# Tail of the second request: row buffers in a pool of their own, gate and up in turn

## The chip, the cores and the metric

The kernel runs on one core of one Trainium2 chip. The core has a matmul engine (PE, with its weight loads shown apart as PEld), three engines for element work (DVE, ACT and POOL) and SP, whose queue issues most of the loads. The metric is the device time of one execution in microseconds, the median of the runs.

## The reference

One layer of a hybrid encoder runs on two requests with the same weights: a prompt P of 512 tokens and a sample S of 1024 tokens, 1024 channels each. The front of the layer (projection, a chunked state-space scan, a long convolution by FFT) isn't touched here. What follows is the tail, the same for both requests:

```python
mix = jnp.concatenate([y_ssd, y_hy], axis=-1) @ w_out          # 2048 -> 1024
h = h + group_rmsnorm(mix, norm_mix_post)
u = group_rmsnorm(h, norm_ffn_pre)
ff = (jax.nn.silu(u @ w_gate) * (u @ w_up)) @ w_down            # 1024 -> 2816 -> 1024
h = h + group_rmsnorm(ff, norm_ffn_post)
gate = jax.nn.sigmoid((group_rmsnorm(h, ple_norm_pre) @ w_ple_gate).astype(f32))
e = (p_l @ w_ple_proj).astype(f32)
h = h + group_rmsnorm((gate * e).astype(dtype), ple_norm_post)
```

Everything is f32, and both requests' outputs are returned.

## The kernel before

**Precision.** Every f32 operand of a product is split into a high part and the rest (`split_w` for weights: ACT makes `whi` at L278, POOL makes `wlo` at L279; `split_ps` for activations: ACT at L311, DVE at L312). A product is three matmuls, `mm3` at L287 to L289: high by high, high by low, low by high. Lines L287 to L289 are shared by all gemms of the tail, so the stages are told apart by the names of the tiles.

**Stages of the tail, in program order.** P: out-projection, FFN, ple (`post` with `ple_norm_post`), with tiles in the pools `tail_u` and `tail_p`. Then S, in groups of 512 tokens, in three pools that follow each other on the right side of SBUF:

- `out_s`: for each of the two groups, `out_group`. It multiplies the 16 row blocks of `mix_s` (read back from DRAM as `mx` tiles by SP, L1172, and split into `mh` and `ml`) with `w_out` in two column halves of 512 (`nch`), 192 matmuls of 512 columns each, and then runs `post`.
- `hid_s`: `gate_up`. The FFN's gate and up products are computed for two column blocks of 128 at a time (a pair; 11 pairs in all) by a scheme of seven block products over four quarter blocks a11, a21, a22, a12 of the weights and sums of them. The first two pairs are done for each group apart (4 calls, 256-wide matmuls, 84 of them to a product), the other nine for both groups at once (168 to a product). The weight blocks come into ten `raw` tiles by SP (L1201), the sums of weight blocks are made on DVE (L1194), gate and up run zipped: one step of the one, one of the other. The results are written as `hid_s` to DRAM (L1267).
- `end_s`: for each group, the down-projection (22 row blocks of `hid_s`, read back as `mx`), its `post`, and the ple.

**The post.** `post` takes the four accumulator tiles of 128 tokens (`acc`): square sum (ACT, L302), reciprocal root (DVE L294, POOL L295), scaling with the gain row (DVE, L1040), residual add (DVE, L1041; the residual is loaded by SP, L1031), store, a second norm (DVE, L319), eight transposes of 128 x 128 a tile on PE (L325), and then a `take`, which makes the seven sums of activation blocks that the scheme wants (`Sums`: DVE L138 for the differences, ACT L311 and DVE L312 for their split into `bh` and `bl`). In P's posts a plain split follows the transposes. The gain rows are loaded by SP (L307).

**What sets the order.** The code is written in order, and the framework places each instruction on its engine's queue by a simulated timeline; `post` is marked urgent, so that it is placed ahead of other work that is ready. Each engine then works its queue off strictly in that order. A tile of a pool can be written when all readers of its former owner are done, and a pool that takes the place of another waits until the tiles there are released. So `hid_s` can't begin before `out_s` is done, and `end_s` not before `hid_s`. Weights of all gemms but gate and up come through six slots `wst` and six each of `whi` and `wlo` (L272).

## Time and profile before

| what | us |
|---|---|
| median of 3 runs | 2953.61 (2950.01 to 2957.2) |
| profiled execution | 2953.8 |
| its span | 2952.0 |
| PE busy | 2693.9 (91% of the span) |
| DVE busy | 1803.0 |
| ACT busy | 1275.2 |
| POOL busy | 1475.6 |
| mean clock granted to PE | 0.953 |

A row of the profile's groups gives the line, the engine, the tiles written and read, the shape and the count, then the busy time and the mean of one in ns, then the idle time of the engine ahead of it and what ended it. In a timeline row the first number is the start in us from the span's start, the second the duration, and the bracket holds the idle time ahead and what ended it. A row of the table by stage gives the stretch, its length, the busy time and instructions of each engine, the granted PE clock, the DMA share and the GB/s moved.

### The profile page before, as it was taken

The page shows a single profiled execution, that of the slowest core. Times are in us where ns is not written, and L with a number is a line of the kernel's source. Part 1 is how long each engine was busy: PE and PEld are TensorE (multiplying, and loading weights), DVE is VectorE, ACT ScalarE, POOL GpSimd, SP SyncE. Part 2 cuts the span into 40 slices and gives each one's busy share as a digit, 9 for nine tenths or more (in the row PEclk, how much of TensorE's full clock was granted, in tenths as well). Part 3 has the DMA queues.
Part 4 walks back from the last instruction along what each step waited for, and adds up shares of the span by engine and source line. Part 5 has one row for each costly group of instructions (what it writes and reads, how often), then busy time and mean ns, then how long its engine had stood idle before and what let it go on. Part 6 is the DMA issues. An engine that isn't in the chain of part 4 may idle for free.

```text
span 2952.0 us, 41577 instructions
## 1 busy us (share of the span) xinstructions
PE 2693.9 (91%) x14696; PEld 2280.1 (77%) x14696; DVE 1803.0 (61%) x2905; ACT 1275.2 (43%) x2442; POOL 1475.6 (50%) x1147
## 2 busy tenths in 40 slices
PE   7999999999999989788888897959489999899998
PEld 5987898788887767677777776748489999878776
DVE  6767996976666968677776833452653333223445
ACT  4534445763234656622223243454543333335453
POOL 4445554434444456555555644533575444435564
PEclk8999999999999999899999998979699999999999
DMA  5544556653435586643333344645332222266755
GB/s 167 176 140 129 159 170 204 197 148 102 120 100 172 184 271 201 222 135 107 100 114 114 96 143 155 217 159 164 116 106 80 77 80 81 80 196 194 237 184 194
DMA packets 430667, 442.28 MB, mean 150 GB/s; under 512 B 26929, under 2 KB 331897, under 8 KB 428155
## 3 DMA queue, kind: packets, MB, share of 16 engines
q1 hardware_dynamic: 344523, 348.39, 39.0%
q10 hardware_dynamic: 79024, 61.88, 6.5%
q0 software_dynamic: 6912, 29.36, 2.5%
q8 instruction: 116, 1.90, 0.3%
q14 instruction: 92, 0.75, 0.1%
HBM read 347.59 MB, written 91.95 MB: 149 GB/s over the span
## 4 chain that ended last, share of the span: by engine, by line
PE 71%; DVE 15%; DMA 5%; issue 3%; POOL 3%; ACT 2%; SPq 0%; ACTq 0%; POOLq 0%; DVEq 0%
PE g L287 18%; PE g L288 18%; PE g L289 18%; PE a L288 3%; PE a L287 3%; PE a L289 3%; DVE b L743 2%; PE a L959 2%; PE a L686 1%; POOL wlo L279 1%; DVE b L678 1%; DVE E L601 1%; PE a L390 1%; PE a L614 1%; POOL rs_t L295 1%
## 5 line engine op out<-in xcount | busy, mean ns | idle before, releaser
L279 POOL TENSOR_TENSOR wlo<-wst,whi 128x512 fp32r<-128x512 f32 (+1 forms) x564 | 827.7, 1476 | 791.3 <-ACT whi L278 737.8
L278 ACT ACTIVATE whi<-wst 128x512 fp32r<-128x512 f32 (+1 forms) x564 | 351.3, 628 | 477.3 <-PE g L288 249.3
L287 PE MATMUL g<-uh,whi 128*128 128x512 f32 (+1 forms) x1232 | 495.1, 402 | 10.9 <-DVE acc L1108 5.5
L289 PE MATMUL g<-uh,wlo 128*128 128x512 f32 (+1 forms) x1232 | 493.6, 401 | 0.0
L288 PE MATMUL g<-ul,whi 128*128 128x512 f32 (+1 forms) x1232 | 493.1, 400 | 0.0
L287 PE MATMUL g<-bh,whi 128*128 128x256 f32 x1056 | 300.0, 285 | 28.6 <-DVE gt L1194 12.3
L289 PE MATMUL g<-bh,wlo 128*128 128x256 f32 x1056 | 299.8, 284 | 1.2 <-POOL wlo L279 1.1
L288 PE MATMUL g<-bl,whi 128*128 128x256 f32 x1056 | 299.5, 284 | 0.0
L312 DVE TENSOR_TENSOR ml<-mx,mh 128x512 fp32r<-128x512 f32 x152 | 118.8, 785 | 286.7 <-ACT mh L311 257.5
L287 PEld LDWEIGHTS g<-uh,whi 128*128 128x128 f32 x1232 | 234.7, 191 | 71.2 <-issue 15.6
L289 PEld LDWEIGHTS g<-uh,wlo 128*128 128x128 f32 x1232 | 234.0, 190 | 54.3 <-issue 5.8
L288 PEld LDWEIGHTS g<-ul,whi 128*128 128x128 f32 x1232 | 234.0, 190 | 53.6 <-issue 6.9
L279 POOL TENSOR_TENSOR wlo<-raw,whi 128x512 fp32r<-128x512 f32 x130 | 174.9, 1356 | 152.4 <-ACT whi L278 138.2
L379 DVE SCALAR_TENSOR_TENSOR cv<-g,cols,cv 128x510 f32<-128x510 f32 (+3 forms) x192 | 193.0, 1006 | 65.1 <-ACT cv L373 63.1
L287 PEld LDWEIGHTS g<-bh,whi 128*128 128x128 f32 x1056 | 203.4, 193 | 30.5 <-DVE gt L1194 13.2
L289 PEld LDWEIGHTS g<-bh,wlo 128*128 128x128 f32 x1056 | 203.8, 193 | 2.0 <-POOL wlo L279 2.0
L288 PEld LDWEIGHTS g<-bl,whi 128*128 128x128 f32 x1056 | 203.9, 193 | 0.0
L295 POOL TENSOR_TENSOR rs_t<-rs_t,nhalf 128x1 f32<-128x1 f32 (+2 forms) x112 | 115.1, 1031 | 168.6 <-DVE rs_t L294 167.2
L287 PE MATMUL g<-whi,uh 128*128 128x264 f32 (+1 forms) x576 | 192.0, 335 | 2.9 <-ACT uh L311 2.1
L311 ACT ACTIVATE mh<-mx 128x512 fp32r<-128x512 f32 x152 | 95.6, 631 | 228.2 <-PE g L288 165.0
L288 PE MATMUL g<-wlo,uh 128*128 128x264 f32 (+1 forms) x576 | 190.6, 331 | 0.0
L289 PE MATMUL g<-whi,ul 128*128 128x264 f32 (+1 forms) x576 | 189.1, 329 | 0.0
(316 smaller groups left out, 6100.4 us busy)
## 6 DMA issues: line engine op xcount, KB each, us to landing
wst<-in_w_in SPq DMA_DIRECT2D x192, 256.0 KB
wst<-in_w_down SPq DMA_DIRECT2D x132, 256.0 KB
wst<-in_w_out SPq DMA_DIRECT2D x96, 256.0 KB
mx<-hid_s SPq DMA_DIRECT2D x88, 256.0 KB
rw<-rows_s SPq DMA_DIRECT2D x32, 512.0 KB
mx<-mix_s SPq DMA_DIRECT2D x64, 256.0 KB
raw<-in_w_gate SPq DMA_DIRECT2D x52, 256.0 KB
raw<-in_w_up SPq DMA_DIRECT2D x52, 256.0 KB
```

What stands on the lines that cost most here:

```text
L278: nc.scalar.activation(hi, w, AF.Copy)
L279: (eng or nc.gpsimd).tensor_tensor(out=lo, in0=w, in1=hi.bitcast(F32), op=ALU.subtract)
L287: nc.tensor.matmul(ps, lh, rh, start=first, stop=False, skip_group_check=shared)
L288: nc.tensor.matmul(ps, lh, rl, start=False, stop=False, skip_group_check=shared)
L289: nc.tensor.matmul(ps, ll, rh, start=False, stop=last, skip_group_check=shared)
L295: nc.gpsimd.tensor_tensor(out=t[:, :w], in0=t[:, :w], in1=self.nhalf[:, :w], op=ALU.pow)
L311: self.nc.scalar.activation(hi, ps, AF.Copy)
L312: self.nc.vector.tensor_tensor(out=lo, in0=ps, in1=hi.bitcast(F32), op=ALU.subtract)
L379: nc.vector.scalar_tensor_tensor(out[:, a:b], ps[:, a + d:b + d], wcol(w), out[:, a:b], ALU.mult, ALU.add)
L390: nc.tensor.transpose(ps[:, j * 128:(j + 1) * 128], srcs[i + j], self.ident)
L743: V.tensor_tensor(out=o, in0=a, in1=b, op=op)
L959: nc.tensor.matmul(ps[:, r], iv[:, r0 + r, c], X[:, r0 + r, c], start=c == 0, stop=c == 1)
```

## The change

A pool `mix_s` with the tiles `mx` (2), `mh` (3) and `ml` (3) is opened on the right side ahead of P's tail and lives to the end; its tiles are the row buffers of both the out-projection and the down-projection. `out_s` is opened beside it, before P's tail, with a `junk` and a `wsum` of its own, and two `stage` tiles in place of four. `stream_gemm` becomes a generator that stops after each column half: the first half of group 0 is written ahead of P's ple. The gemm of group 1 is as before behind the post of group 0 in the code; `out_group` and `out_post` are apart now. In `gate_up`, the two single pairs of group 0 have their `wsum`, `gt` and `sc` in the tiles of `mix_s`; the others have them in `hid_s`. Gate and up are computed in turn: the last two of the seven steps of one product run beside the first two of the next. The weights come through `wst` (six slots, shared with the other gemms), the product is written over the `gt` tile, and each weight sum is made right after its inputs' last use. In `take` the differences read the PSUM tile for the second half of the rows, and eight ACT copies fall away in all. `end_s` has no `mx`, `mh` and `ml` of its own.

```diff
     def take(self, ps, k, t):
-        x = self.stage[t, k] = K.T(self.pool, [128, 4, 128], "stage")
-        nc.scalar.activation(x, ps, AF.Copy)
-        if k == 0 or t < 2:
+        if t < 2:
+            x = self.stage[t, k] = K.T(self.pool, [128, 4, 128], "stage")
+            nc.scalar.activation(x, ps, AF.Copy)
             return
...
+        if k == 0:
+            w = self.stage[t, 0] = K.T(self.pool, [128, 4, 128], "wsum")
+            diff(w, ps, b11)
+            put(1, b11)
+            put(5, w)
+            return
+        w = self.stage[t, 0]
+        put(3, ps)
+        diff(w, ps, w)
...
     def stream_gemm(self, rows, nk, wsrc, evac):
...
             for t in ORDER:
                 evac(nch, t, pss[t])
+            yield
...
-            a11, a21, a22, a12 = (self.T(pool, [128, 4, 128], "raw") for _ in range(4))
+            a11, a21, a22, a12 = (self.raw_w(w[k:k + 512, c * 128:(c + 1) * 128].rearrange(
+                "(k p) m -> p k m", p=128)) for c, k in ((m, 0), (m + 1, 0), (m + 1, 512), (m, 512)))
...
             mm(1, X, a11, True)
             r1 = copy()
+            s1 = add(a21, a22, ALU.add)
             yield
-            s1 = add(a21, a22, ALU.add)
             mm(5, Z, s1, True)
+            s2 = add(s1, a11, ALU.subtract)
             yield
...
-            for _ in zip(product(I["w_gate"][0], m, gs, gate), product(I["w_up"][0], m, gs, mul)):
-                pass
-
-        for gs, ms in (([0], (0, 2)), ([1], (0, 2)), ([0, 1], range(4, NF, 2))):
-            for m in ms:
-                pair(m, gs)
+            yield product(I["w_gate"][0], pool, m, us, gate)
+            yield product(I["w_up"][0], pool, m, us, mul)
+
+        old = None
+        for job in jobs:
+            for p in pair(*job):
+                for i in range(5):
+                    next(p)
+                    if old and i < 2:
+                        next(old)
+                old = p
...
+        with self.pool("mix_s", side="right") as mp, ExitStack() as right:
+            pm = tags(mp, ("mx", 2), ("mh", 3), ("ml", 3))
+            tr = right.enter_context(self.pool("out_s", side="right"))
+            po = pm | tags(tr, ("acc", 4), ("row", 2), ("t4", 2), ("junk", 1), ("stage", 2), ("wsum", 1))
+            with self.pool("tail_u") as tu, self.pool("tail_p") as tp:
...
+                u = self.ffn(P, 0, pl, u)
+                acc = self.new_acc(po)
+                out = self.out_group(S, 0, po, acc)
+                next(out)
+                self.ple_post(P, 0, pl, self.ple(P, 0, pl, u))
...
+            next(out)
...
+                us = [self.out_post(S, 0, po, acc)]
+                acc = self.new_acc(po)
+                for _ in self.out_group(S, 1, po, acc):
+                    pass
+                us.append(self.out_post(S, 1, po, acc))
+                right.close()
+                with self.pool("hid_s", side="right") as tr:
+                    ph = pb | tags(tr, ("wsum", 3), ("sc", 5), ("gt", 6))
+                    pe = pb | {"wsum": pm["mx"], "gt": pm["mh"], "sc": pm["ml"]}
...
+                with self.pool("end_s", side="right") as tr:
+                    pe = pb | tags(tr, ("row", 3), ("t4", 3), ("junk", 1), ("mst", 2))
```

Lines of the changed kernel that are named here are moved: L287 to L289 are L292 to L294, L319 is L324, L325 is L330, L272 is L277, L307 is L312, L1031 is L1036, L1172 is L1178.

How the change moves instructions is shown at three places. The first is PE at the end of P's down-projection, where P's FFN post begins (`g_16278` is the down-projection's PSUM tile, `acc_13667` the post's first tile, `g_16495` the ple's). Before:

```order
L289 MATMUL g_16278<-whi_16299,hl_16196 128x512
L325 MATMUL a_16410<-ident_105,acc_13667 128x128 x4
L287 MATMUL g_16495<-whi_16499,uh_16355 128x512
L288 MATMUL g_16495<-wlo_16500,uh_16355 128x512
L325 MATMUL a_16417<-ident_105,acc_13667 128x128 x4
```

And now, where `g_16284` is the down-projection, `g_16501` and `g_16502` are S's out-projection and `acc_13673` is the post's first tile:

```order
L294 MATMUL g_16284<-whi_16305,hl_16202 128x512
L292 MATMUL g_16501<-whi_16517,mh_16505 128x512
L293 MATMUL g_16501<-wlo_16518,mh_16505 128x512
...
L292 MATMUL g_16502<-whi_16619,mh_16607 128x512
L293 MATMUL g_16502<-wlo_16620,mh_16607 128x512
L330 MATMUL a_16416<-ident_105,acc_13673 128x128 x4
L294 MATMUL g_16501<-whi_16619,ml_16608 128x512
```

64 matmuls of S's out-projection stand between the down-projection and the post's first transposes, where there was none. The same is so in the post of group 0, whose transposes stand among the matmuls of group 1's out-projection: 76, 112 and 132 of them ahead of the first, the third and the fourth tile's.

The second place is PE at the end of group 1's out-projection, where its post follows. Before, with the post's four `acc` tiles and the first matmul of `gate_up`:

```order
L289 MATMUL g_18238<-whi_18595,ml_18584 128x512
L325 MATMUL a_18692<-ident_105,acc_17841 128x128 x4
L325 MATMUL a_18699<-ident_105,acc_17841 128x128 x4
L325 MATMUL a_18718<-ident_105,acc_17843 128x128 x4
L325 MATMUL a_18725<-ident_105,acc_17843 128x128 x4
L325 MATMUL a_18764<-ident_105,acc_17842 128x128 x4
L325 MATMUL a_18771<-ident_105,acc_17842 128x128 x4
L325 MATMUL a_18779<-ident_105,acc_17844 128x128 x4
L325 MATMUL a_18786<-ident_105,acc_17844 128x128 x4
L287 MATMUL g_18825<-bh_17655,whi_18826 128x256
```

And now, where the out-projection ends with `ml_18577`:

```order
L294 MATMUL g_18231<-whi_18588,ml_18577 128x512
L292 MATMUL g_18808<-bh_17658,whi_18809 128x256
...
L294 MATMUL g_18914<-bh_17663,wlo_18990 128x256
L330 MATMUL a_18685<-ident_105,acc_17834 128x128 x4
L330 MATMUL a_18692<-ident_105,acc_17834 128x128 x4
L292 MATMUL g_18808<-bh_17661,whi_18935 128x256
...
L294 MATMUL g_18808<-bh_17661,wlo_18936 128x256
L330 MATMUL a_18711<-ident_105,acc_17836 128x128 x4
...
L294 MATMUL g_18914<-bh_17661,wlo_19079 128x256
L330 MATMUL a_18752<-ident_105,acc_17835 128x128 x4
L330 MATMUL a_18759<-ident_105,acc_17835 128x128 x4
```

84 matmuls of group 0's first pair stand ahead of the first transposes, 12 more ahead of the second tile's, 24 more ahead of the third tile's; the fourth's follow at once.

The third place is SP around the start of the down-projection: gain rows, the residual `t` and the rows `mx` of `hid_s`. Before:

```order
L272 DMA wst_24419<-in_w_down 128x512
L307 DMA row_25237<-in_norm_ffn_post 128x1024
L307 DMA row_25239<-in_ple_norm_pre 128x1024
L307 DMA row_26451<-in_norm_ffn_post 128x1024
L1031 DMA t_4897_25241<-h_s 128x1024
L1031 DMA t_4898_25243<-h_s 128x1024
L1031 DMA t_4919_25302<-h_s 128x1024
L1172 DMA mx_24161<-hid_s 128x512
L1172 DMA mx_24167<-hid_s 128x512
```

And now:

```order
L1178 DMA mx_24172<-hid_s 128x512
...
L277 DMA wst_24334<-in_w_down 128x512
L312 DMA row_25152<-in_norm_ffn_post 128x1024
L312 DMA row_25154<-in_ple_norm_pre 128x1024
L312 DMA row_26366<-in_norm_ffn_post 128x1024
L1036 DMA t_4817_25156<-h_s 128x1024
L1036 DMA t_4818_25158<-h_s 128x1024
L1036 DMA t_4839_25217<-h_s 128x1024
L1178 DMA mx_24178<-hid_s 128x512
```

The first five rows of group 0 (`mx_24076` to `mx_24172`) are issued among the loads of `gate_up`'s weights; the sixth, `mx_24178`, stands behind the three gain rows and the three residual tiles.

More of the change, by code (lines that the diff above doesn't have):

```diff
@@ L1166, in streamed, with rows @@
     def streamed(self, pool, src, g):
-        def rows(nch, k0):
+        def rows(k0):
             out = []
@@ L1241, in product @@
             sink(1, 1, Z, r3)
+            tt(a12, a12, s2, ALU.subtract)
             yield
@@ L1400, in build @@
-        self.apool = self.pools["x"][0]
-        with self.pool("blocks") as tb:
-            pl = {t: (tb, t, 14) for t in ("bh", "bl")}
-            def phase(pool, *tags):
-                return pl | {t: (pool, t, n) for t, n in tags}
-            with self.pool("out_s", side="right") as tr:
-                po = phase(tr, ("mx", 2), ("mh", 3), ("ml", 3), ("acc", 4), ("row", 2), ("t4", 2), ("stage", 4))
-                po["junk"] = po["wsum"] = po["mx"]
-                us = [self.out_group(S, g, po, lambda: Sums(self, po)) for g in range(2)]
-            with self.pool("hid_s", side="right") as tr:
-                self.gate_up(S, phase(tr, ("raw", 10), ("wsum", 3), ("sc", 4), ("gt", 5), ("up", 5)), us)
-            with self.pool("end_s", side="right") as tr:
-                pe = phase(tr, ("mx", 4), ("mh", 4), ("ml", 4), ("row", 3), ("t4", 3), ("junk", 1), ("mst", 2))
-                pe |= {"acc": pe["bl"], "ga": pe["bh"]}
-                self.wide_tail = True
-                vs = [self.down_group(S, g, pe, lambda: Quarters(
-                    *[[self.T(pe, [128, 4, 256], t, F32R) for _ in range(4)] for t in ("bh", "bl")]))
-                    for g in range(2)]
-                for g in range(2):
-                    self.ple_post(S, g, pe, self.ple(S, g, pe, vs[g]))
@@ new lines, in tags @@
+        def tags(pool, *sizes):
+            return {t: (pool, t, n) for t, n in sizes}
+        with self.pool("mix_s", side="right") as mp, ExitStack() as right:
[3 more added lines that the diff above has]
+            with self.pool("tail_u") as tu, self.pool("tail_p") as tp:
+                pl = tags(tu, ("et", 2), ("hh", 4), ("hl", 4), ("t4", 2), ("uh", 2), ("ul", 2))
+                pl |= tags(tp, ("acc", 4), ("mst", 1), ("row", 2), ("junk", 1))
+                pl["mx"] = pl["t4"]
+                pl["ga"] = pl["acc"]
+                pt = self.ple_in(pl, [(S, 1)], True)
+                mix = self.mix_in(P, 0, pl, 0, 8)
+                self.ple_proj(pl, [(S, 1)], pt)
+                acc = self.new_acc(pl)
+                self.outproj(P, 0, pl, acc, 0, mix)
+                pt = self.ple_in(pl, [(P, 0), (S, 0)])
+                u = self.outproj(P, 0, pl, acc, 8, self.mix_in(P, 0, pl, 8, 8), lambda: self.new_u(pl, 4))
+                self.ple_proj(pl, [(P, 0), (S, 0)], pt)
+                u = self.ffn(P, 0, pl, u)
[3 more added lines that the diff above has]
+                self.ple_post(P, 0, pl, self.ple(P, 0, pl, u))
+            self.apool = self.pools["x"][0]
+            next(out)
+            with self.pool("blocks") as tb:
+                pb = pm | tags(tb, ("bh", 14), ("bl", 14))
+                po |= pb
+                us = [self.out_post(S, 0, po, acc)]
+                acc = self.new_acc(po)
+                for _ in self.out_group(S, 1, po, acc):
+                    pass
+                us.append(self.out_post(S, 1, po, acc))
[3 more added lines that the diff above has]
+                    pe = pb | {"wsum": pm["mx"], "gt": pm["mh"], "sc": pm["ml"]}
+                    both = dict(enumerate(us))
+                    self.gate_up(S, [(p, m, {g: both[g] for g in gs}) for p, gs, ms in (
+                        (pe, [0], (0, 2)), (ph, [1], (0, 2)), (ph, [0, 1], range(4, NF, 2))) for m in ms])
+                with self.pool("end_s", side="right") as tr:
+                    pe = pb | tags(tr, ("row", 3), ("t4", 3), ("junk", 1), ("mst", 2))
+                    pe |= {"acc": pe["bl"], "ga": pe["bh"]}
+                    self.wide_tail = True
+                    vs = [self.down_group(S, g, pe, lambda: Quarters(
+                        *[[self.T(pe, [128, 4, 256], t, F32R) for _ in range(4)] for t in ("bh", "bl")]))
+                        for g in range(2)]
+                    for g in range(2):
+                        self.ple_post(S, g, pe, self.ple(S, g, pe, vs[g]))
```

98 lines of the change are left out of this document (42 added, 56 removed).

## The prediction

> **What bounds the kernel now.** I read the page first, for the busy share of each engine and for the chain of waits.
>
> ```profile
> span 2952.0 us, 41577 instructions
> PE 2693.9 (91%) x14696; PEld 2280.1 (77%) x14696; DVE 1803.0 (61%) x2905; ACT 1275.2 (43%) x2442; POOL 1475.6 (50%) x1147
> PE 71%; DVE 15%; DMA 5%; issue 3%; POOL 3%; ACT 2%; SPq 0%; ACTq 0%; POOLq 0%; DVEq 0%
> ```
>
> PE is busy for 91% of the span and holds 71% of the chain; the rest are places where the chain leaves PE for DVE, a DMA or POOL. The two kernels issue the same instructions in the same order on every engine up to about 1640 us, so only the places behind that matter. The second view gives the busy time by stage there. Its stages are: the end of P's FFN and P's ple; out-projection of group 0; its post; the first matmuls behind it; a steady stretch of 512-wide matmuls; the post of group 1; the four column pairs for one group each; the nine pairs for both groups; the turn to the down-projection.
>
> ```profile
> core 0: us, PE busy (x) PEld busy (x) DVE busy (x) ACT busy (x) POOL busy (x), PEclk, DMA share, GB/s
> 1769.50:1841.40 71.90, 54.78 (x225) 42.13 (x224) 26.18 (x33) 25.96 (x45) 31.42 (x29) 0.83 0.45 154
> 1841.40:1938.50 97.10, 91.63 (x384) 72.98 (x384) 42.72 (x44) 44.02 (x79) 51.51 (x41) 0.98 0.62 198
> 1938.50:1976.40 37.90, 7.68 (x33) 6.28 (x32) 30.91 (x42) 22.67 (x41) 12.67 (x14) 0.55 0.50 166
> 1976.40:1981.00 4.60, 4.55 (x13) 3.69 (x14) 2.03 (x3) 1.36 (x4) 0.00 (x0) 0.62 0.35 114
> 2000.00:2060.00 60.00, 60.00 (x259) 48.35 (x258) 16.33 (x22) 25.76 (x45) 24.62 (x20) 1.00 0.57 180
> 2067.60:2105.70 38.10, 7.74 (x34) 6.32 (x33) 28.87 (x42) 21.65 (x39) 10.20 (x13) 0.60 0.29 103
> 2105.70:2218.30 112.60, 92.70 (x676) 90.39 (x677) 67.61 (x78) 49.96 (x102) 87.18 (x61) 0.86 0.40 114
> 2224.00:2571.50 347.50, 347.50 (x2974) 347.33 (x2972) 119.04 (x152) 124.98 (x213) 165.46 (x124) 1.00 0.25 76
> 2571.50:2590.10 18.60, 0.04 (x1) 0.00 (x0) 2.35 (x2) 1.28 (x3) 1.26 (x1) 0.56 0.74 268
> ```
>
> The full rate comes from the two rows at clock 1.00: 60.00/259 = 0.232 us for a 512-wide matmul, 347.50/2974 = 0.117 us for a 256-wide one. A post has 32 transposes of 128 columns; I count them at the 256-wide rate at most, 3.7 us. What each stage takes above its matmuls at these rates is what the change can reach:
>
> - A, P's end: 71.9 - 192 x 0.232 - 3.7 = 23.7
> - B, out-projection of group 0: 97.1 - 384 x 0.232 = 8.0
> - C, its post: 37.9 - 3.7 = 34.2, and 4.6 - 13 x 0.232 = 1.6 for the slow matmuls behind it
> - D, post of group 1: 38.1 - 3.7 = 34.4
> - E, the single pairs: 112.6 - 672 x 0.117 = 34.0
> - F, the turn to down: 18.6, and 1.6 again behind it
>
> Together 156.1 us. The long stage from 2224 to 2571 has nothing to give: PE is busy all of it. So the bound is PE where it has work, and the DVE-ACT-POOL chain of three posts, the weight preparation of the single pairs and one pipeline refill where it has none. The third view, PE's own timeline, shows how a post spends its time.
>
> ```profile
> 1781.38 1.12 PE L325 MATMUL a<-ident,acc 128*128 128x128 f32 x4 [11.86 <-DVE acc L319]
> 1849.94 0.62 PE L287 MATMUL g<-whi,mh 128*128 128x512 f32 x1 [4.09 <-ACT mst L1331]
> 1951.24 3.67 PE L325 MATMUL a<-ident,acc 128*128 128x128 f32 x16 [12.61 <-DVE acc L319]
> 1962.91 1.94 PE L325 MATMUL a<-ident,acc 128*128 128x128 f32 x8 [8.00 <-DVE acc L319]
> 1967.10 1.94 PE L325 MATMUL a<-ident,acc 128*128 128x128 f32 x8 [2.25 <-DVE acc L319]
> 1976.45 0.80 PE L287 MATMUL g<-whi,mh 128*128 128x512 f32 x1 [7.41 <-ACT mh L311]
> 2078.27 3.67 PE L325 MATMUL a<-ident,acc 128*128 128x128 f32 x16 [10.53 <-DVE acc L319]
> 2089.62 1.94 PE L325 MATMUL a<-ident,acc 128*128 128x128 f32 x8 [7.68 <-DVE acc L319]
> 2093.82 1.94 PE L325 MATMUL a<-ident,acc 128*128 128x128 f32 x8 [2.25 <-DVE acc L319]
> 2105.66 0.58 PE L287 MATMUL g<-bh,whi 128*128 128x256 f32 x1 [9.90 <-ACT whi L278]
> 2590.13 0.80 PE L287 MATMUL g<-whi,mh 128*128 128x512 f32 x1 [18.59 <-ACT mh L311]
> ```
>
> From a post's start to its first transposes PE waits 10.5 to 12.6 us, the third tile's come 22 to 24 us after the start, the fourth's 26 to 29 us, and the next stage's first matmul 38 us. All these waits end with DVE or ACT.
>
> **The change part by part.** (1) *A and B.* The first column half of group 0's out-projection, 192 matmuls, stands between P's down and P's ple. In the new order 64 of them come before the first transposes: 64 x 0.232 = 14.9 us against a wait of 11.9 us, so that wait goes. Between the later transposes stand 12 to 24 matmuls each against DVE work and the loads of h_p; I leave 5 us of A's 23.7. Bounds: 0, or 23.7 - 14.9 = 8.8 if only the first wait is covered.
>
> ```profile
> wst<-in_w_out SPq DMA_DIRECT2D x96, 256.0 KB
> mx<-mix_s SPq DMA_DIRECT2D x64, 256.0 KB
> ```
>
> The moved half brings 16 rows and 16 weight blocks, 32 such loads of 256 KB, for its 44.5 us of matmuls, 188 GB/s, ahead of the ple's on SP; in B the same work is fed at 198 GB/s and a DMA share of 0.62, and A has room below that (154 GB/s, 0.45), so I add nothing for it. B keeps the second half and loses the 4.09 us wait for ACT at P's end at best: 4 of 8.0 left, bounds 0 and 8.
>
> (2) *C.* The GEMM of group 1 stands beside the post of group 0: 76 matmuls (17.6 us) ahead of its first transposes, where 12.6 us are waited now; 112 (26.0 us) ahead of the third tile's, due at 24 us; 132 (30.6 us) ahead of the fourth's, due at 29 us. Every one is due before PE gets there by 1.6 to 5 us. But the GEMM needs row splits on DVE at the same time as the post:
>
> ```profile
> L312 DVE TENSOR_TENSOR ml<-mx,mh 128x512 fp32r<-128x512 f32 x152 | 118.8, 785 | 286.7 <-ACT mh L311 257.5
> L1040 DVE SCALAR_TENSOR_TENSOR acc<-acc,rs_t,row 128x1024 f32<-128x1024 f32 x4 | 6.0, 1532 | 1.5 <-POOL rs_t L295 1.5
> L1041 DVE TENSOR_TENSOR t<-acc,t 128x1024 f32<-128x1024 f32 x4 | 5.9, 1487 | 2.2 <-DMA t<-in_x_sample 2.2
> ```
>
> Beside the 30.9 us that DVE is busy in C come 16 row splits of 0.785 us, 12.6 us. So the post's DVE work stretches from 38 to at most 51 us, all of it under 384 matmuls, 89 us. I leave 6 us for transposes that come late; bounds 2 and 16.6 (34.2 - 17.6, only the first wait covered). The 1.6 us at slow clock goes with the gap.
>
> (3) *D and E together.* The first two pairs of group 0 (336 matmuls) may run beside the post of group 1. The order gives less: 84 of them (9.8 us) before the first transposes, then 12, 8 and 16: 120 matmuls, 14.0 us, before the last. The fourth tile's transposes ended 28 us after the start (2093.82 + 1.94 against 2067.6), and PE's queue is in order, so PE waits about 28 - 14.0 - 3.7 = 10 us there. Then 552 matmuls are left, 64.6 us. Their weights go through POOL:
>
> ```profile
> L279 POOL TENSOR_TENSOR wlo<-raw,whi 128x512 fp32r<-128x512 f32 x42 | 59.5, 1448 | 21.6 <-DMA raw<-in_w_gate 13.3 <-ACT whi L278 8.3
> L279 POOL TENSOR_TENSOR wlo<-wsum,whi 128x512 fp32r<-128x512 f32 x19 | 28.8, 1524 | 17.1 <-ACT whi L278 15.6 <-DVE up L1194 1.3
> L1194 DVE TENSOR_TENSOR raw<-raw,wsum 128x512 f32<-128x512 f32 x8 | 12.9, 1637 | 5.5 <-POOL wlo L279 5.5
> L1194 DVE TENSOR_TENSOR wsum<-wsum,raw 128x512 f32<-128x512 f32 x10 | 13.3, 1328 | 0.0
> L1194 DVE TENSOR_TENSOR wsum<-wsum,raw 128x512 f32<-128x512 f32 x16 | 11.0, 689 | 17.8 <-POOL wlo L279 17.8
> ```
>
> A step of a single pair is 12 matmuls, 1.40 us, and needs one POOL split of 1.45 to 1.52 us. So these 46 steps go at POOL's pace, 46 x 1.45 = 66.7 us, and I add 8 us for sums that come late, in place of the 34 us of now: gate and up in turn have each sum made a step before it is split. Stage D and E then take 28 + 66.7 + 8 = 103 us against 38.1 + 112.6 = 150.7; above the matmuls (82.3) about 21 are left, 25 with a post that is slowed by the weight sums. Bounds: 14 (POOL never late, post 28 us) and 42 (below).
>
> (4) *F.* Five mx rows of group 0 are loaded and three of them split while gate_up still runs. Behind the last gate_up matmul stand 18 + 24 matmuls on rows 0 to 4: 42 x 0.232 = 9.7 us. Row 5 is queued on SP behind three row loads and three h_s loads, which wait for the pool of gate_up to be given back:
>
> ```profile
> 2576.91 0.33 SPq L307 DMA_DIRECT2D row<-in_norm_ffn_post  x1
> 2580.24 16.34 SPq L1172 DMA_DIRECT2D mx<-hid_s  x9
> 2589.45 2.19 ACT L311 ACTIVATE mh<-mx 128x512 fp32r<-128x512 f32 x4 [17.30 <-DMA mx<-hid_s]
> ```
>
> Those six loads are issued 5.4 us after the last matmul now and the first split of a row follows at 18 us. If that stands, PE runs dry at 9.7 us and waits 9 more, then 1.6 at slow clock: 11 left of 20.2, bounds 3 (the load in the middle) and 20.
>
> (5) *Costed at nothing.* Eight ACT copies less (sums read from PSUM): ACT was not the last wait in C. The result written over gt, and the weights of gate_up in six shared slots in place of ten: covered by the nine double pairs, where a product takes 168 x 0.117 = 19.7 us and POOL is busy 165 of 347 us; the price without that cover is a rival. Two mx slots and three splits in the down-projection where four of each were: 2 us, and 3 us for the other pools' waits.
>
> Sum: left 5 + 4 + 6 + 25 + 11 + 5 = 56 of 156, so 100 us less. The profiled execution is 2953.8 us (span 2952.0), 0.2 above the median of 2953.61: forecast 2854 us. With the lower bounds 0 + 0 + 2 + 14 + 3 it is 2817, with the upper 8.8 + 8 + 16.6 + 42 + 20 + 5 it is 2898.
>
> **The rivals.** *R1, only the first wait of each post is covered.* The transposes stand in PE's fixed order; if the post runs later than its place, PE waits there as now. Then the cover is 14.9 + 17.6 + 14.0 us, half of E (17) and 9.7 in F: 73 us less, 2881. For it: D's transposes stand at 14 us and are due at 28. Against: in A and C they stand behind their due time.
>
> *R2, DVE bounds the posts.* The two L1194 rows show the same sum at 1.33 us beside POOL and 0.69 in the stage of the double pairs. A post has some 30 operations on DVE that read two SBUF tiles; at 0.65 us more each, 20 us, paid in full in D and by half in C: 2854 + 30 = 2884. For it: weight sums and POOL splits now run beside the post of group 1. Against: the posts of now hold some of this already, with 1.53 and 1.49 us for L1040 and L1041.
>
> The Trainium skill (page "SBUF — State Buffer", section "SBUF: two separate sides") says that a VectorE operation with two SBUF inputs and a GpSimd operation that reads SBUF take one port pair in turn, and the loser waits for the whole instruction. The rows agree in size (0.64 to 0.95 us more, a POOL split being 1.45), and by that rule R2 is this kernel's way to it; a sum that reads PSUM on one side would escape.
>
> *R3, slower: the double pairs lose their cover.* Each of their 18 products waits for its load, because four blocks do not fit beside the previous product's four in six slots.
>
> ```profile
> 2101.77 2.03 SPq L1201 DMA_DIRECT2D raw<-in_w_gate  x4
> ```
>
> From this issue to the first matmul at 2105.66 are 3.9 us, the split that the third matmul needs takes 1.4 more, the slow clock 1.6: 6.9 x 18 = 124 us, 2978. It decides from 5.6 us a product, where it eats the 100. Against: the stage moves 76 GB/s at a DMA share of 0.25, and two slots are always ahead.
>
> *R4, the change does not do what it says:* a pool still waits for the other's release and the stages follow each other, 2950 to 2956. Against: the new order has the matmuls of one stage ahead of the other's transposes.
>
> *R5, nearly all is hidden:* 2 + 2 + 2 + 14 + 9 left, 127 less, 2827.
>
> **How the numbers follow.** Forecast (2835 to 2872) 0.53; R1 0.15; R2 0.11; R5 0.13; R3 0.04; R4 0.02; in between 0.02. The likeliest gives 2854. The range takes in R1, R2 and R5 and the bounds of the sum: 2815 to 2900, leaving out R3, R4 and small tails. What a measurement of this kernel can tell from no change is about 0.2%, 6 us: faster 0.94, same 0.02, slower 0.04.
>
> **What would show it.** In the new profile: PE busy share up to about 94%; no gap over 3 us ahead of the transposes in A and C; in D a gap of some 10 us in all, ended by DVE acc L324, and single pairs ending about 103 us after the out-projection; then a stretch of some 350 us with PE at 100%; a gap of some 9 us behind the last of rows 0 to 4, ended by the DMA of mx from hid_s. R1 would show gaps of 8 us or more ahead of the third tile's transposes, R2 post operations of 2 us and over on DVE, R3 PE under 95% in the double pairs. The forecast is wrong if A and C together still hold over 25 us of gaps, or D and E take over 125 us.

## The result and the profile after

The changed kernel takes 2902.85 us (median of 4 runs, 2901.39 to 2904.5) against 2951.81 us before: a ratio of 0.983, 95% interval 0.981 to 0.985. It is 49 us faster, half of the 100 forecast, and 3 us above the upper end of the range. The page of the changed kernel, first the busy time and then the chain of waits:

```profile
span 2902.5 us, 41421 instructions
PE 2699.4 (93%) x14696; PEld 2280.2 (79%) x14696; DVE 1844.2 (64%) x2905; ACT 1266.0 (44%) x2434; POOL 1492.9 (51%) x1147
PE 70%; DVE 15%; DMA 5%; issue 4%; POOL 3%; ACT 2%; SPq 0%; ACTq 0%; POOLq 0%; DVEq 0%
```

The table by stage of the changed kernel, cut at its own borders: P's end and P's ple with the first half of group 0's out-projection; the second half; the out-projection of group 1 beside the post of group 0; the post of group 1 with its fill; the rest of the single pairs; the double pairs; the rows 0 to 4 of the down-projection and the gap behind them; the rest.

```profile
core 0: us, PE busy (x) PEld busy (x) DVE busy (x) ACT busy (x) POOL busy (x), PEclk, DMA share, GB/s
1765.50:1869.90 104.40, 96.33 (x416) 76.54 (x415) 44.17 (x48) 45.27 (x79) 53.16 (x44) 0.97 0.56 186
1869.90:1924.80 54.90, 48.03 (x193) 36.71 (x193) 33.53 (x30) 24.15 (x44) 32.20 (x27) 0.97 0.63 207
1924.80:2030.80 106.00, 97.23 (x417) 76.97 (x416) 65.99 (x79) 58.45 (x106) 54.92 (x44) 0.97 0.60 196
2030.80:2073.00 42.20, 24.28 (x154) 22.04 (x152) 35.34 (x41) 25.23 (x50) 30.57 (x24) 0.81 0.40 128
2073.00:2159.80 86.80, 73.74 (x554) 70.79 (x553) 56.54 (x71) 41.35 (x87) 60.87 (x44) 0.93 0.34 103
2159.80:2528.30 368.50, 364.90 (x3044) 361.00 (x3043) 146.40 (x161) 125.52 (x217) 177.59 (x128) 1.00 0.28 82
2528.30:2547.00 18.70, 10.22 (x44) 7.81 (x42) 4.52 (x5) 5.35 (x9) 8.12 (x6) 0.87 0.71 244
2547.00:2902.50 355.50, 336.21 (x1444) 270.40 (x1444) 157.40 (x179) 163.41 (x288) 181.02 (x145) 0.97 0.60 198
```

The last post is the clearest: the stretch from group 1's gemm to its last transposes is 42.2 us, where it was 28 without a fill. DVE is busy for 35.3 of these 42.2 us. The same operations are longer than before. Here are the three 128x1024 operations of this post, scale, second norm and residual add, in the kernel before:

```profile
L1040 DVE SCALAR_TENSOR_TENSOR acc<-acc,rs_t,row 128x1024 f32<-128x1024 f32 x4 | 5.1, 1284 | 1.5 <-POOL rs_t L295 1.5
L319 DVE SCALAR_TENSOR_TENSOR acc<-t,rs_t,row 128x1024 f32<-128x1024 f32 x4 | 5.1, 1282 | 0.9 <-POOL rs_t L295 0.9
L1041 DVE TENSOR_TENSOR t<-acc,t 128x1024 f32<-128x1024 f32 x4 | 4.9, 1224 | 1.9 <-DMA t<-in_x_sample 1.9
```

And now (L1045, L324 and L1046), then other operations of DVE beside them:

```profile
L1045 DVE SCALAR_TENSOR_TENSOR acc<-acc,rs_t,row 128x1024 f32<-128x1024 f32 x4 | 7.1, 1787 | 2.2 <-POOL rs_t L300 2.2
L324 DVE SCALAR_TENSOR_TENSOR acc<-t,rs_t,row 128x1024 f32<-128x1024 f32 x4 | 6.8, 1701 | 3.3 <-POOL rs_t L300 3.3
L1046 DVE TENSOR_TENSOR t<-acc,t 128x1024 f32<-128x1024 f32 x4 | 5.8, 1456 | 0.0
L317 DVE TENSOR_TENSOR bl<-stage,bh 128x512 fp32r<-128x512 f32 x4 | 5.4, 1367 | 0.0
L317 DVE TENSOR_TENSOR bl<-a,bh 128x512 fp32r<-128x512 f32 x1 | 0.7, 676 | 0.0
L317 DVE TENSOR_TENSOR bl<-wsum,bh 128x512 fp32r<-128x512 f32 x2 | 1.4, 676 | 0.0
```

The mean of 1.37 us for the split `bl` with `stage` as its input is the work of one operation: three of the four took 0.68 us, as the splits with `wsum` (also in SBUF) and with `a` (PSUM) did, and one took 3.44. In the timeline, DVE and POOL lie like this beside that one:

```profile
2056.73 3.44 DVE L317 TENSOR_TENSOR bl<-stage,bh 128x512 fp32r<-128x512 f32 x1
2057.12 1.27 POOL L284 TENSOR_TENSOR wlo<-wst,whi 128x512 fp32r<-128x512 f32 x1
2058.36 1.26 POOL L284 TENSOR_TENSOR wlo<-mx,whi 128x512 fp32r<-128x512 f32 x1
```

Its 0.68 us and the two POOL splits beside it (2.53) make 3.2 of the 3.44. The whole trace of the changed kernel behind 1765.5 us shows what decides: of DVE's 128x512 sums and splits with both inputs in SBUF, 106 start while a split of POOL is running, and they take 1.68 us in the median; the other 230 take 0.67 to 0.70, all but 4. The 100 with an input in PSUM take 0.67 to 0.70 throughout, though 58 of them lie beside a split of POOL. POOL's splits are longer too in this stretch:

```profile
L284 POOL TENSOR_TENSOR wlo<-wst,whi 128x512 fp32r<-128x512 f32 x9 | 15.5, 1734 | 0.6 <-ACT whi L283 0.5
```

The idle time ahead of an operation stands behind the second bar and isn't part of its duration: the instructions themselves have become longer. PE's longest wait in this stretch isn't for the post's tiles but for the fill itself:

```profile
PE g L292 <- DVE ml L1201: 9.4, 1, 9.4
```

A matmul of the fill needs a PSUM tile that DVE has yet to read (`ml<-g,ml`), and this read stands behind the post's operations in DVE's queue: PE's last matmul ended at 2055.3 us and DVE came to the read at 2064.3. The transposes of the last two tiles stand behind it on PE.

The out-projection's post of group 0 has the longer operations too:

```profile
L1046 DVE TENSOR_TENSOR t<-acc,t 128x1024 f32<-128x1024 f32 x4 | 8.1, 2028 | 0.0
L324 DVE SCALAR_TENSOR_TENSOR acc<-t,rs_t,row 128x1024 f32<-128x1024 f32 x4 | 8.0, 2001 | 0.0
L1045 DVE SCALAR_TENSOR_TENSOR acc<-acc,rs_t,row 128x1024 f32<-128x1024 f32 x4 | 7.0, 1783 | 1.5 <-POOL rs_t L300 1.5
```

### The profile page after: what moved, and what is told of

Read it like the earlier page. It is cut to its first block, busy times and chain, and to the rows that moved or that the text cites. A ratio compares the mean times of both kernels' runs of the same rounds, so it can differ in the third digit from the quotient of the medians.

```text
span 2902.5 us, 41421 instructions
## 1 busy us (share of the span) xinstructions
PE 2699.4 (93%) x14696; PEld 2280.2 (79%) x14696; DVE 1844.2 (64%) x2905; ACT 1266.0 (44%) x2434; POOL 1492.9 (51%) x1147
## 4 chain that ended last, share of the span: by engine, by line
PE 70%; DVE 15%; DMA 5%; issue 4%; POOL 3%; ACT 2%; SPq 0%; ACTq 0%; POOLq 0%; DVEq 0%
PE g L292 18%; PE g L294 17%; PE g L293 17%; PE a L292 3%; PE a L293 3%; PE a L294 3%; DVE b L748 3%; PE a L964 2%; POOL wlo L284 2%; PE a L691 1%; DVE b L683 1%; DMA mx<-mix_s 1%; DVE E L606 1%; PE a L395 1%; PE a L619 1%
## 5 line engine op out<-in xcount | busy, mean ns | idle before, releaser
L284 POOL TENSOR_TENSOR wlo<-wst,whi 128x512 fp32r<-128x512 f32 (+1 forms) x694 | 1026.7, 1487 | 967.4 <-ACT whi L283 889.2
L283 ACT ACTIVATE whi<-wst 128x512 fp32r<-128x512 f32 (+1 forms) x694 | 433.5, 629 | 752.7 <-PE g L293 429.3
L292 PE MATMUL g<-uh,whi 128*128 128x512 f32 (+1 forms) x1232 | 495.4, 402 | 10.8 <-DVE acc L1113 5.5
L294 PE MATMUL g<-uh,wlo 128*128 128x512 f32 (+1 forms) x1232 | 493.8, 401 | 0.0
L292 PE MATMUL g<-bh,whi 128*128 128x256 f32 x1056 | 296.8, 287 | 25.6 <-DVE ml L1201 9.4
L294 PE MATMUL g<-bh,wlo 128*128 128x256 f32 x1056 | 296.9, 283 | 3.0 <-POOL wlo L284 3.0
L292 PEld LDWEIGHTS g<-uh,whi 128*128 128x128 f32 x1232 | 234.9, 191 | 70.3 <-issue 16.2
L294 PEld LDWEIGHTS g<-uh,wlo 128*128 128x128 f32 x1232 | 234.0, 190 | 54.2 <-issue 5.8
L317 DVE TENSOR_TENSOR ml<-mx,mh 128x512 fp32r<-128x512 f32 x152 | 129.6, 855 | 221.6 <-ACT mh L316 221.5
L292 PEld LDWEIGHTS g<-bh,whi 128*128 128x128 f32 x1056 | 199.4, 191 | 32.2 <-DVE ml L1201 9.8
L294 PEld LDWEIGHTS g<-bh,wlo 128*128 128x128 f32 x1056 | 201.7, 191 | 3.2 <-POOL wlo L284 3.2
L292 PE MATMUL g<-whi,uh 128*128 128x264 f32 (+1 forms) x576 | 190.3, 332 | 1.4 <-ACT et L1343 1.4
L294 PE MATMUL g<-whi,ul 128*128 128x264 f32 (+1 forms) x576 | 187.4, 326 | 0.0
L292 PE MATMUL g<-whi,mh 128*128 128x512 f32 x380 | 155.9, 410 | 12.4 <-ACT mh L316 11.1
```

The costliest lines, as they stand in the source:

```text
L283: nc.scalar.activation(hi, w, AF.Copy)
L284: (eng or nc.gpsimd).tensor_tensor(out=lo, in0=w, in1=hi.bitcast(F32), op=ALU.subtract)
L292: nc.tensor.matmul(ps, lh, rh, start=first, stop=False, skip_group_check=shared)
L294: nc.tensor.matmul(ps, ll, rh, start=False, stop=last, skip_group_check=shared)
L317: self.nc.vector.tensor_tensor(out=lo, in0=ps, in1=hi.bitcast(F32), op=ALU.subtract)
```

## The experiments

The next table is the measure for all runs. "Lost" is the length of a stage less its matmuls at 0.2317 us (512 columns) and 0.1168 us (256), and 3.7 us for a post's transposes. A+B reaches from P's down-projection to the end of group 0's out-projection, C to the end of group 1's, D+E to the end of the single pairs, "pairs" is the double pairs, "rest" goes on to the end of the span. The kernels are the changed one with the edit told below. The time at which P's down-projection ends, with the same work ahead of it, lies between 1764.4 and 1770.8 us over the profiled executions, so stages are compared and not times of day. Each row is one profiled execution. Where a run's edit doesn't touch a stage, the column still varies: A+B from 20.1 to 22.4, C from 13.2 to 14.8, D+E from 45.2 to 48.3, the rest from 34.5 to 37.7; and the kernel before had medians of 2951.8 to 2954.0 us in the sets of runs. A difference of 2 or 3 us between two rows is not resolved.

| run | us | ratio to before (95%) | A+B | C | D+E | pairs | rest | sum |
|---|---|---|---|---|---|---|---|---|
| before | 2951.8 | | 32.0 | 36.4 | 68.1 | 0.3 | 39.9 | 176.7 |
| forecast | 2854 | | 9 | 6 | 25 | 0 | 36 | 76 |
| changed | 2902.9 | 0.983 (0.981 to 0.985) | 22.4 | 13.3 | 46.8 | 11.1 | 37.7 | 131.3 |
| e1 | 2906.1 | 0.984 (0.983 to 0.986) | 21.6 | 13.2 | 51.9 | 8.6 | 36.1 | 131.4 |
| e2 | 2891.1 | 0.980 (0.978 to 0.981) | 21.3 | 13.6 | 36.1 | 10.9 | 35.1 | 116.9 |
| e3 | 2880.6 | 0.976 (0.974 to 0.977) | 20.7 | 13.9 | 31.9 | 7.5 | 34.5 | 108.6 |
| e4 | 2898.7 | 0.982 (0.981 to 0.984) | 21.5 | 8.4 | 45.2 | 10.9 | 37.2 | 123.3 |
| e5 | 2880.2 | 0.977 (0.975 to 0.978) | 20.5 | 13.3 | 28.5 | 8.8 | 36.0 | 107.2 |
| e6 | 2898.5 | 0.982 (0.981 to 0.984) | 20.1 | 13.7 | 46.5 | 11.0 | 35.5 | 127.0 |
| e7 | 2892.7 | 0.980 (0.978 to 0.982) | 20.9 | 13.4 | 43.8 | 4.7 | 37.5 | 120.2 |
| e8 | 2895.8 | 0.982 (0.980 to 0.984) | 22.0 | 14.8 | 48.3 | 11.3 | 31.4 | 127.8 |
| e9 | 2888.0 | 0.978 (0.977 to 0.980) | 21.2 | 13.2 | 40.0 | 5.9 | 35.1 | 115.4 |
| e10 | 2910.5 | 0.986 (0.984 to 0.987) | 32.0 | 10.7 | 46.8 | 11.0 | 35.2 | 135.8 |
| e11 | 2864.9 | 0.970 (0.969 to 0.972) | 22.1 | 7.6 | 30.3 | 0.1 | 31.4 | 91.5 |
| e12 | 2844.9 | 0.964 (0.963 to 0.966) | 7.7 | 6.0 | 29.8 | 0.1 | 28.8 | 72.5 |

**e1: no fill beside the post of group 1.**

```diff
-                        (pe, [0], (0, 2)), (ph, [1], (0, 2)), (ph, [0, 1], range(4, NF, 2))) for m in ms])
+                        (ph, [0], (0, 2)), (ph, [1], (0, 2)), (ph, [0, 1], range(4, NF, 2))) for m in ms])
```

> The two pairs of group 0 take their tiles from the pool of gate_up again, so they start only when the post of group 1 is done; all else as in the changed kernel (2903 us; the post of group 1 and the single pairs take 128.5 us there). Theory K (the work that was put beside the post stretches it: DVE and POOL wait for each other and DVE has more to do): the post goes back to some 38 us, the pairs take some 90 us behind it, 125 to 135 us together, so the time stays within 8 us of 2903. Theory F (the fill is worth the PE time that it covers, only less than foreseen): 14 us of matmuls and the weight preparation beside the post are lost, 2920 us or more.

The time can't be told from the changed kernel's. The post without a fill needs 27.5 us to its last transposes, and its operations are at the durations of before:

```profile
L324 DVE SCALAR_TENSOR_TENSOR acc<-t,rs_t,row 128x1024 f32<-128x1024 f32 x4 | 5.1, 1281 | 0.9 <-POOL rs_t L300 0.9
L1045 DVE SCALAR_TENSOR_TENSOR acc<-acc,rs_t,row 128x1024 f32<-128x1024 f32 x4 | 5.0, 1283 | 1.5 <-POOL rs_t L300 1.5
L1046 DVE TENSOR_TENSOR t<-acc,t 128x1024 f32<-128x1024 f32 x4 | 4.9, 1224 | 1.3 <-DMA t<-in_x_sample 1.3
```

So the fill that this part of the change is built for gives 5 us in D+E, and the pairs lose 2.5 more beside it (their matmuls step at 0.118 us, and at 0.117 in e1): theory K holds, and F's 14 us are not there.

**e2: the fill's weight splits on DVE.** `split_w` takes an engine for the low part.

```diff
-                h, l = self.split_w(x)
+                h, l = self.split_w(x, nc.vector if list(us) == [0] else None)
```

> The low parts of the weights of group 0's two first pairs (28 splits) are made on DVE in place of POOL. Theory K1 (contention of DVE and POOL): the 128x1024 operations of group 1's post (scale, add, norm) go from 1.5 to 1.8 us back to below 1.4 us, the last transposes end 34 us or less after the gemm in place of 42, and the time falls by 5 to 12 us. Theory K2 (the amount of work in DVE's queue, no contention): 28 x 0.69 = 19 us more on DVE, the post ends later than 42 us and the time rises by 5 to 19 us.

12 us less, though DVE has 28 more instructions. The post's operations, in the stretch up to the last transposes, and the moved splits on DVE:

```profile
L324 DVE SCALAR_TENSOR_TENSOR acc<-t,rs_t,row 128x1024 f32<-128x1024 f32 x4 | 5.1, 1276 | 0.6 <-POOL rs_t L300 0.4
L1045 DVE SCALAR_TENSOR_TENSOR acc<-acc,rs_t,row 128x1024 f32<-128x1024 f32 x4 | 5.0, 1281 | 0.7 <-POOL rs_t L300 0.7
L1046 DVE TENSOR_TENSOR t<-acc,t 128x1024 f32<-128x1024 f32 x4 | 4.9, 1213 | 0.0
L284 DVE TENSOR_TENSOR wlo<-wst,whi 128x512 fp32r<-128x512 f32 x9 | 6.0, 680 | 0.0
```

They are at 1.28 and 1.21 us again, and a split that took POOL 1.73 us there takes DVE 0.68. The last transposes end 35.6 us after the gemm in place of 42.2 (34 or less were expected), and the fill's wait for its PSUM read is 4.0 us in place of 9.4. K1 holds. The order on PE isn't quite the same, as the framework places everything anew: 96 of the fill's matmuls stand ahead of the first transposes, where 84 did. A split also comes sooner from DVE than from POOL, which would help without any contention; but in the changed kernel PE's waits that end with a split of POOL are 4.2 us in D+E, and none in A+B and C.

**e3: the same splits as a copy on ACT.** The kernel leaves out the low parts of these weights.

```diff
+        if eng == "act":
+            nc.scalar.activation(lo, w, AF.Copy)
```

> The low parts of the same 28 weight splits are made by a plain copy on ACT (so they hold the rounded weight and not the rest: the two first pairs of group 0 are not the reference's). This takes POOL's work away from beside the post and adds none to DVE. Theory K1 (contention): the post's 128x1024 operations below 1.4 us, last transposes 30 to 35 us after the gemm, 8 to 15 us less. Theory K2 (DVE's own amount of work): the operations as long as in the changed kernel, the time within 4 us of 2903.

22 us less, more than K1 expected: D+E lose 31.9 us. The post's operations are at 1.28, 1.28 and 1.23 us, the last transposes 35.4 us after the gemm, no earlier than in e2. So POOL's splits no longer set the post's length. What does isn't isolated: the copies bring ACT more work (29.5 us busy of 35.4), and the transposes stand at other places among PE's matmuls than in e2. The 4 us between e2 and e3 in D+E may be DVE's own work or that order; 3.6 more of the 22 are in the pairs.

**e4: the splits of group 1's out-projection on DVE,** with the same parameter handed through `stream_gemm` and `load_w`.

```diff
-        return self.stream_gemm(self.streamed(pool, q.mix, g), 16, self.I["w_out"][0], self.keep(acc))
+        return self.stream_gemm(self.streamed(pool, q.mix, g), 16, self.I["w_out"][0], self.keep(acc),
+                                self.nc.vector if g == 1 else None)
```

> The low parts of w_out for group 1 (32 splits), which run beside the post of group 0, are made on DVE in place of POOL. Theory K1: the post's 128x1024 operations, 1.8 to 2.0 us in the changed kernel, go below 1.4 us; the stage of group 1's out-projection (107.6 us, 14.9 of them without matmul work) gets 4 to 8 us shorter. Theory K2: 32 x 0.69 = 22 us more on DVE, beside 66.6 us that it is busy of 107.6; the stage gets longer by 3 to 10 us.

C loses 8.4 us in place of 13.3, its operations are at 1.28, 1.28 and 1.22 us. The time falls by 4 us, which the intervals don't separate; the stage does.

**e5: all single pairs' splits on DVE.**

```diff
-                h, l = self.split_w(x)
+                h, l = self.split_w(x, nc.vector if len(us) == 1 else None)
```

> As e2, but the low parts of the weights of all four single pairs (56 splits, group 1's too) are made on DVE. In e2 (2891 us) the stretch from the last transposes to the end of the single pairs takes 82.6 us for 64.6 us of matmuls. If POOL's splits, at 1.45 us for a step of 1.40 us, and their contention with the weight sums set that stretch, it falls to 68 to 74 us and the time to 2877 to 2884. If DVE's amount of work sets it (56 us of 82.6 busy, 19 more by this), or the chain from product to product, it stays within 3 us of 82.6 or grows, and the time is 2889 or more.

The stretch behind the last transposes falls from 82.6 (e2) to 75.1 us, one us above what the first case expected, and the time to 2880. D+E lose 28.5 us; the forecast had 25.

**e6: the down-projection's rows ahead of its post's loads.** The gain rows and the first two residual tiles are loaded in `down_group`, behind the gemm in the code, and handed to `post`.

```diff
+        pre = None
+        if g == 0:
+            pre = [self.gain_row(pool, "row", n) for n in ("norm_ffn_post", "ple_norm_pre")] + [{}]
...
+        self.post(pool, acc, "norm_ffn_post", q.h1, g * 512, q.h2, "ple_norm_pre", v, pre=pre)
```

> The gain rows and residual tiles of the down-projection's first post are asked for behind the first rows of hid_s, so that one 512 KB row load is left ahead of the sixth row in SP's queue in place of six loads of 512 KB. If the 8.1 us gap of PE at the start of the down-projection comes from that queue (the row was issued at 2537.9 and landed at 2546.3), the row lands 3 to 4 us after its issue, the gap falls to 1 to 3 us and the time by 4 to 7 us. If the release of gate_up's pool sets it, the gap stays above 6 us and the time within 3 us of 2903.

SP's queue and the first split of the sixth row, first of the changed kernel, then of e6:

```profile
2534.66 0.33 SPq L312 DMA_DIRECT2D row<-in_norm_ffn_post  x1
2535.99 1.88 SPq L1036 DMA_DIRECT2D t<-h_s  x3
2537.91 0.95 SPq L1178 DMA_DIRECT2D mx<-hid_s  x2
2546.33 0.63 ACT L316 ACTIVATE mh<-mx 128x512 fp32r<-128x512 f32 x1 [6.31 <-DMA mx<-hid_s]
```

```profile
2531.64 0.33 SPq L312 DMA_DIRECT2D row<-in_norm_ffn_post  x1
2532.07 0.38 SPq L1182 DMA_DIRECT2D mx<-hid_s  x1
2536.92 0.63 ACT L316 ACTIVATE mh<-mx 128x512 fp32r<-128x512 f32 x1 [5.54 <-DMA mx<-hid_s]
2537.61 0.50 PE L292 MATMUL g<-whi,mh 128*128 128x512 f32 x1 [1.37 <-ACT mh L316]
2547.80 0.60 PE L292 MATMUL g<-whi,mh 128*128 128x512 f32 x1 [3.54 <-ACT mh L316]
```

From issue to split it is 4.9 us in place of 8.4, and the issue itself comes 6.7 us after the last matmul of the double pairs in place of 9.4. PE's first gap is 1.4 us; in the changed kernel it is 7.7:

```profile
2547.01 0.79 PE L292 MATMUL g<-whi,mh 128*128 128x512 f32 x1 [7.71 <-ACT mh L316]
```

A second gap of 3.5 us comes up for the rows behind it. The rest loses 2 us less and the time falls by 4 us, neither of which can be told from the spread. The queue was the cause of the gap, but half of its worth moves on.

**e7: overlap of three steps.**

```diff
-                for i in range(5):
+                for i in range(4):
                     next(p)
-                    if old and i < 2:
+                    if old and i < 3:
                         next(old)
```

> Gate and up overlap by three steps of seven in place of two. The stage of the nine double pairs takes 368 us in the changed kernel and 353.5 before; at each product's border PE stands still 0.5 us or more behind a DVE read of the product's PSUM tile (18 borders). If those waits come from having too little of the other product beside a read, the stage falls by 4 to 9 us. If the loss is the slower steps themselves (0.118 us a matmul against 0.117) or the weights, it stays within 3 us.

The double pairs take 362.0 us in place of 368.5 and the time falls by 10 us. The row of the changed kernel at one product's border, and the stage in e7 with PE busy all of it but 0.8 us:

```profile
2192.16 0.39 PE L292 MATMUL g<-bh,whi 128*128 128x256 f32 x1 [0.26 <-DVE gt L1201]
```

```profile
2159.20:2521.20 362.00, 361.21 (x3044) 360.21 (x3042) 136.76 (x162) 126.67 (x218) 172.89 (x128) 1.00 0.28 84
```

A product accumulates on a PSUM tile that DVE has just read; with too little of the other product beside it PE waits for that read. From one matmul to the next, 37 steps in this stage take 0.18 us or more, together 7.8 us above 0.117 each, and 5.4 of these end with a read of `gt` by DVE; in e7 three such steps are left, with 1.1 us. The mean of the others, 0.118 us in both against 0.117 before, stays.

**e8: more split rows for group 1's down-projection.** `own` holds two more `mh` and `ml`, used by every second row.

```diff
-                out.append([self.T(pool, [128, 512], t, F32R) for t in ("mh", "ml")])
+                out.append([self.T(pool | own if k % 2 else pool, [128, 512], t, F32R) for t in ("mh", "ml")])
```

> The down-projection of group 1 has two more tiles each for the split rows (mh and ml: five in place of three). Beside the post of group 0 PE waits 6.8 us for row splits there (three gaps, 1.8, 3.2 and 1.8 us, against 3.0 us in the kernel before). If the number of tiles sets these waits, they fall to 3 us or less and the time by 3 to 5 us. If DVE is late with its splits, since the post's operations and POOL's splits hold it up, they stay above 5 us and the time within 2 us.

PE's waits in the down-projection of group 1, in the changed kernel and in e8:

```profile
PE g L294 <- DVE ml L317: 6.8, 3, 3.2
```

```profile
PE g L294 <- DVE ml L317: 2.0, 3, 1.0
```

The number of tiles sets these waits. The rest loses 31.4 us in place of 37.7, some 3 to 6 us less than the runs without this edit.

**e9: no fill, splits of all single pairs on DVE** (e1 and e5 together).

> e1 and e5 together: group 0's first pairs wait for the post of group 1 again, and the low parts of all single pairs are made on DVE. With the splits on POOL, taking the fill away cost 3 us. If contention with POOL was what ate the fill's worth, taking it away costs more without POOL: 10 to 16 us against e5 (2880 us), 2890 to 2896. If the fill is worth little in any case, because DVE has the same work to do in either order, it costs 5 us or less.

8 us above e5, between the two expectations; D+E lose 40.0 in place of 28.5, and the pairs give 2.9 back. Without POOL's splits the fill is worth 11.5 us in its own stage, with them 5. So of the 14 us hoped for, contention took some 6, and some 3 weren't there in either case.

**e10: the first half of group 0's out-projection behind P's ple.**

```diff
-                acc = self.new_acc(po)
-                out = self.out_group(S, 0, po, acc)
-                next(out)
                 self.ple_post(P, 0, pl, self.ple(P, 0, pl, u))
+                acc = self.new_acc(po)
+                out = self.out_group(S, 0, po, acc)
+                next(out)
```

> The first column half of group 0's out-projection is written behind P's ple again, so that it no longer fills P's FFN post; all else as in the changed kernel. There P's end, the ple and the out-projection of group 0 lost 20.6 us above their matmuls, against 31.7 in the kernel before. If the fill in P's post is worth the 11 us between the two, the time rises by 8 to 13 us (2911 to 2916). If contention ate it as it did in the post of group 1, it rises by 4 us or less.

7.6 us slower, just under what was expected for a fill that is worth its 11 us (A+B is back at 32.0, as before the change; C is 2.6 better). This fill works, as far as it goes.

**e11: e4 to e8 together.**

> The five edits that were faster one at a time, together: low parts of the single pairs on DVE (-23 us), overlap of three steps (-10), row and residual loads behind the first rows of hid_s (-4), two more tiles each for the split rows of group 1's down-projection (-7), low parts of w_out for group 1 on DVE (-4). If each takes away a loss of its own, the sum holds: -40 to -50, 2853 to 2863. If they share a loss (DVE's amount of work), less than 35 comes.

38 us less than the changed kernel, 2 us short of the sum's lower edge: the five edits gave 48 us one at a time. The 10 us between may be losses that they share, or lie in the spread of the five single figures.

**e12: e11, and the splits of group 0's out-projection on DVE too.**

```diff
-                                self.nc.vector if g == 1 else None)
+                                self.nc.vector)
```

> As e11, with the low parts of w_out on DVE for group 0 too (32 splits beside P's FFN post and P's ple post). If contention with POOL also stretches P's two posts, P's end and the out-projection of group 0 (20.6 us lost) get 3 to 8 us shorter and the time is below e11 by as much; if DVE's work (26 to 33 us busy of each of these stages) is the limit, it is at e11's or up to 5 us above.

20 us below e11, far more than the 3 to 8 expected, and 109 us below the kernel before: 2844.9 us. A+B lose 7.7 us in place of 22.1. PE's waits for the row splits of S and P there (`mh`, `ml`, `ul`) are 13.7 us in e11 and 4.4 in e12. The cause shows on P's ple post beside the second half of group 0's out-projection. In the changed kernel, split rows and scale:

```profile
L317 DVE TENSOR_TENSOR ml<-mx,mh 128x512 fp32r<-128x512 f32 x15 | 15.2, 1021 | 16.9 <-ACT mh L316 16.9
L1045 DVE SCALAR_TENSOR_TENSOR acc<-acc,rs_t,row 128x1024 f32<-128x1024 f32 x4 | 8.8, 2190 | 0.0
```

And in e12, where some lines have moved (L1045 is L1048):

```profile
L317 DVE TENSOR_TENSOR ml<-mx,mh 128x512 fp32r<-128x512 f32 x14 | 9.6, 689 | 5.9 <-ACT mh L316 5.7
L1048 DVE SCALAR_TENSOR_TENSOR acc<-acc,rs_t,row 128x1024 f32<-128x1024 f32 x4 | 5.1, 1280 | 0.4 <-POOL rs_t L300 0.4
L284 DVE TENSOR_TENSOR wlo<-wst,whi 128x512 fp32r<-128x512 f32 x17 | 11.4, 686 | 4.1 <-ACT whi L283 4.1
```

## Why the prediction was wrong

The forecast's account of the bound held: PE where it has work, the posts, the single pairs and one refill where it has none. Some 100 of the 156 us could indeed be reached, but not by this kernel: e12 ends with 72.5 us lost in the measure of the table, where the forecast had 76, and it needs edits that the forecast didn't reckon with. What failed was the price of the overlap in the kernel as it was changed: the steps took the instructions of DVE and POOL, and the post that is made of them, at their durations of before. By steps:

(1) A and B, 9 us left by the forecast, 22.4 measured. The 64 matmuls ahead of the first transposes cover that wait as worked out (0.8 us left of 11.9). But row splits and weight splits now run beside each of P's two posts, and POOL and DVE hold each other up: e12 moves POOL's splits and 7.7 are left. The step had no term for it: "I leave 5 us of A's 23.7".

(2) C, 6 left, 13.3 measured. The step counted DVE's work (30.9 and 12.6 us) and let it stretch to 51 us, at the durations of before. They were 1.8 to 2.0 us where 1.2 to 1.5 were taken. Without POOL's splits (e4) it is 8.4.

(3) D and E, 25 left, 46.8 measured. This is the term that failed most. The post's chain was taken at its old 28 us, with 4 us for the sums; it took 42.2, so 42.2 - 14.0 - 3.7 = 24.5 us were lost where 10 were reckoned: PE stood still for 17.9 of them, and the rest are matmuls at a granted clock of 0.81. The forecast had a gap of some 10 us that ends with the post's `acc` (L324); there is one of 9.4 us, but it ends with DVE's read of the fill's own product, and the waits for `acc` are 1.8 us. That the size agrees is luck: the step took the fill to run ahead without DVE.

The rest of the single pairs took 86.8 us where 75 were reckoned, 46 splits at POOL's pace and 8 us for late sums. POOL was busy for 60.9 of the 86.8 us, so its pace alone doesn't give them; 9 us of the stretch are matmuls at a clock of 0.93. D and E together took 129.0 us, over the 125 that the prediction had named as its limit. Of the 22 us by which the term was short, e5 gives 18 back by moving 56 splits from POOL to DVE. The fill itself, 120 matmuls, was reckoned for its full 14.0 us; it is worth 5, or 11.5 without contention (e1, e9).

(4) F, a gap of 9 us forecast, 7.7 measured, by the queue of SP that was named (e6).

(5) "Costed at nothing": gate and up in turn cost 11.1 us in the double pairs, where 0 was taken. Some 8 of them are single long steps at the products' borders, of which e7 leaves 1. They come not from the weights in six slots, which R3 had feared: 5.4 us end with the PSUM read between two steps of one product, which the zip had covered with the other product's step. The other 3 are the longer mean step. For the rest 36 us were forecast and 37.7 measured. The three split tiles, priced at 2 us together with the two `mx` tiles, cost 4.8 us of PE's waits that go in e8; the `mx` tiles weren't tested.

The rival R2 had the mechanism, a chance of 0.11, and 2884 us. Its place was too narrow and its price too low: it put 20 us in D and half of it in C, and left A and B out. Measured by what goes when the splits leave POOL, it is 18 us in D and E, 5 in C and 14 in A and B: 37 us. With the 11 us of the double pairs these are 48 of the 55 us between forecast and measurement in the measure of the table. R1 holds in part: in e3, with these splits off both POOL and DVE, the last transposes still end 35.4 us after the gemm, against 27.5 without a fill.

The rule of the Trainium skill (page "SBUF — State Buffer", section "SBUF: two separate sides") was weighed in the prediction and given too little. It says that a VectorE operation with two SBUF inputs and a GpSimd operation that reads SBUF take the port pair in turn, whole instruction by whole instruction. The trace of the changed kernel agrees: the operations with a PSUM input kept 0.68 us beside POOL's splits, and of the ones with two SBUF inputs those that started inside a split of POOL took 1.68 in the median, the others 0.69.

What stays open: the mean step of 0.118 us in the double pairs, some 3 us, at a granted clock of 1.00 in every run: it is 0.1178 to 0.1180 in some runs, and 0.1164 to 0.1173 in e1, e3, e5, e9, e11 and e12, and none of them isolates it. And the last 28 us of D and E, which no run goes below: with the fill gone (e9) or the fill's splits off POOL (e3) more is lost.
